# Starting places of the split weight tiles in a two-layer encoder trunk

## The chip, the core and the metric

The kernel runs on one core of a Trainium2 chip. The time is the device time of one execution in microseconds (us); the smaller the better. The core has five engines that run side by side and wait for each other through semaphores: TensorE (PE; its weight loads are shown as PEld), VectorE (DVE), ScalarE (ACT), GpSimd (POOL) and SyncE (SP), which here issues DMAs. TensorE reads its operands from SBUF, the on-chip working memory of 128 partitions, and writes to PSUM. An address below is a byte address within an SBUF partition; it is the same in all partitions.

## The reference

The reference computes a two-layer encoder on 512 tokens of width 1024 in float32. Layer 0 (A) mixes with a gated matrix memory (mLSTM, 4 heads of 192) beside cross-attention to 256 memory tokens; layer 1 (B) mixes with chunked band attention (12 heads of 64, keys and values from a projection made once after layer 0) beside the same kind of cross-attention. After each mixer comes a gated MLP of width 2816 with a causal convolution of width 3. Cut to the parts that name the weights:

```python
def conv_ffn(h, w_up, conv_w, conv_b, w_down):
    u, g = jnp.split(h @ w_up, 2, axis=-1)
    g = causal_dwconv(g, conv_w, conv_b)
    return (jax.nn.silu(g) * u) @ w_down

for l in range(DEPTH):
    h = rmsnorm(x, norm_mix_g[l])
    if l < N_A_LAYERS:
        proj = h @ a_w_in[a]        # q, k, v, o, gates, q_mem -> mlstm_chunkwise
    else:
        proj = h @ b_w_in[bl]       # q, q_mem -> band_attention over k_pad, v_pad
    mem_out = memory_attention(q_mem, mem, mem_w_kv[l])
    x = x + jnp.concatenate([mix_out, mem_out], axis=-1) @ w_out
    x = x + conv_ffn(rmsnorm(x, norm_ffn_g[l]), ...)
    if l == N_A_LAYERS - 1:
        ks_, vs_ = jnp.split(rmsnorm(x, kv_norm_g) @ w_kv, 2, axis=-1)
return rmsnorm(x, final_g)
```

## The kernel before

**Products in three parts.** Activations are kept with the features on the partitions, 512 tokens in the free dimension. Every operand of a product is split into a high part, rounded to the type fp32r, and a low part, the rest. A product is then three matmuls into one PSUM tile: high by high, low by high and high by low. `mm3` (L167 to L171) issues them; L169 reads the high part of the stationary operand with the high part of the moving one, L170 the high part with the low part of the moving one, and L171 the low part of the stationary one. Each matmul loads its stationary operand, 128 by 128, anew.

**Weight tiles.** `load` (L136) brings a block of a weight matrix of up to 128 x 1024 into a buffer `wr`, by a DMA of SP's queue. `parts` (L148) takes a buffer `wh` and a buffer `wl`, and `split` (L129) fills them: L130 casts `wr` into `wh` on ACT, and L131 subtracts `wh` from `wr` into `wl` on DVE. `halves` (L155) takes the same two buffers without filling them, where the order of the casts is written out by hand. `weights` (L160) is `load` and `parts` together. Each of the tags `wr`, `wh` and `wl` has three buffers that are used in turn, 4096 bytes a partition; a tile is taken from the start of its buffer. In the built program the first `wh` buffer starts at byte 188480, the first `wl` buffer at byte 200768, behind them come the tags `rb` (rows of the norms) and `bias`. There are 208 pairs of `wh` and `wl`.

**Who reads the tiles.** In most products the weights are the stationary operand: `project` (L173: `wh[:, k, :]` for each of 8 blocks k, 512 bytes apart), `OutProjection.part` (L614), `down_products` (L741), the key products of the memory (L353), and in the second form of the MLP `products` (L766) and `wide_products` (L780, its lines L784 and L785), which read halves of tiles that `split_up` and `split_sums` (L889, L892) made by `parts`. In `value_columns` (L979), `value_products` (L360) and the last product of the kernel (L1446 to L1466) the weights are the moving operand. In `value_columns` a tile holds two row blocks of 384 columns, or of 392 where the eight gate columns are loaded with them. The MLP also makes forms of weights in buffers of the tag `u` (L869), which has 57 buffers of 2048 bytes.

**Order.** PE, ACT and DVE run in an order written out by hand in the first stage (L422) and in the second form of the MLP (L799); elsewhere the order comes from the generators that `weave` (L200) interleaves, a filler of projections beside the steps of an attention. Tiles are planned by tag: a buffer is free again when the last reader of its former tile is done, and the engine that writes it waits for that.

Of the kernel before, what the change touches and what calls it, by code (L numbers as in the profile page):

```python
# [10 lines left out]
F32R = mybir.dt.float32r  # L11
# [5 lines left out]
P = 128  # L17
D = 1024
# [37 lines left out]
def trunk(  # L56
# [30 lines left out]
    def sb(tag, shape, dtype=F32):  # L87
        count[0] += 1
        return pool.tile(shape, dtype, tag=tag, name=f"{tag}{count[0]}", bufs=bufs[tag])

    def ps(tag):
        count[0] += 1
        return psum.tile([P, S], F32, tag=tag, name=f"p{tag}{count[0]}", bufs=pbufs[tag])
# [35 lines left out]
    def split(hi, lo, src, on_act=True, pinned=False):  # L129
        high = A.copy(hi, src) if on_act else V.tensor_copy(hi, src)  # L130
        low = V.tensor_tensor(out=lo, in0=src, in1=f(hi), op=ALU.subtract)  # L131
        if pinned:
            pin(high)
            pin(low)

    def load(src, a, b, extra=None):  # L136
# [8 lines left out]
            nc.sync.dma_start(raw[:, :, b:], extra)  # L145
        return raw

    def parts(raw, pinned=False):  # L148
        _, a, b = raw.shape
        hi = sb("wh", [P, D], F32R)[:, : a * b].rearrange("p (a b) -> p a b", a=a)  # L150
        lo = sb("wl", [P, D], F32R)[:, : a * b].rearrange("p (a b) -> p a b", a=a)
        split(hi, lo, raw, pinned=pinned)
        return hi, lo

    def halves(raw):  # L155

        _, a, b = raw.shape
        return [sb(tag, [P, D], F32R)[:, : a * b].rearrange("p (a b) -> p a b", a=a) for tag in ("wh", "wl")]

    def weights(*args):  # L160
        return parts(load(*args))

    def rows(w, c0, n, k0=0, k1=None):
        k1 = k1 if k1 is not None else w.shape[0] // P
        return w[k0 * P : k1 * P, c0 : c0 + n].rearrange("(k p) c -> p k c", p=P)
# [85 lines left out]
    class Norm:  # L251
# [14 lines left out]
        def finish(self):  # L266


            parts = [sb("t", [P, S], F32R) for _ in range(2)]
            split(*parts, self.acc)  # L270
            yield 7.4
            o = ps("sc")
            for i, part in enumerate(parts):
                nc.tensor.matmul(o, onesr, part, start=i == 0, stop=i == 1)
            v, r, t = sb("rb", [P, S]), sb("t", [P, S]), sb("t", [P, S])
            A.activation(t, o, AF.Ln, scale=1.0 / D, bias=eps)
            V.tensor_scalar(v, o, 1.0 / D, EPS, op0=ALU.mult, op1=ALU.add)
            A.activation(r, t, AF.Exp, scale=-0.5)
            A.activation(t, r, AF.Square)
            yield 4  # L280
            V.scalar_tensor_tensor(t, t, -0.5, v, op0=ALU.mult, op1=ALU.mult)
            self.row = sb("rb", [P, S])
            V.scalar_tensor_tensor(self.row, t, 1.5, r, op0=ALU.add, op1=ALU.mult)
# [138 lines left out]
    with tc.manual_schedule(engines={mybir.EngineType.PE, mybir.EngineType.Activation, mybir.EngineType.DVE}):  # L422
# [9 lines left out]
        for q in range(KT // 2 + 1):  # L432
            if q < KT // 2:
# [6 lines left out]
                hi, lo = sb("u", [P, S], F32R), sb("u", [P, S], F32R)  # L440
# [32 lines left out]
        for j in range(KT):  # L473
            G.dma_start(xspill[j], xT[j])
        norm.spread()
        vws1.append(halves(vraw1[1]))
        A.copy(vws1[1][0], vraw1[1])
        vo = two_banks("mm", "sc")
        value_products(vo, *vws1[0], 0)
        keep(1, 0, ko, A.copy)  # L480
        raw = value_weights(1, 0)
        vw = [halves(raw)]
        A.copy(vw[0][0], raw)
        x_scaled(0)
# [783 lines left out]
    for j in range(KT):  # L1268
        wh, wl = weights(rows(ffn_w_down[0], j * P, P, FT - LAST, FT), LAST, P)
        o = ps("mm")  # L1270
# [175 lines left out]
    for hf in range(2):  # L1446
# [6 lines left out]
        for Ts, pieces in groups:  # L1453
            for c in pieces:
                if c.start:
                    os_[Ts[0]] = ps("mm")
                for u in range(n):
# [3 lines left out]
                    wh, wl = ws[u]  # L1461
# [61 lines left out]
```

## Time and profile before

| | |
|---|---|
| median of 3 runs | 1194.86 us (1194.71 to 1195.16) |
| profiled execution | 1195.72 us, its span 1194.0 us |
| mean granted TensorE clock | 0.999 |
| instructions in the span | 18184 |
| matmuls | 6719 |

The span runs from the first to the last instruction of the profiled execution; the execution's own time also holds what lies around it. Lines such as L169 are line numbers of the kernel before. A group reads: line, engine, operation, output tile<-input tiles by the program's names, shape, count, then busy time and the mean ns of one, then the idle time of the engine just before and what ended it. The answers about a tile give the shortest, median and longest duration in ns of each kind of instruction that writes or reads it, and when the first and the last one started. The timeline gives start and length in us of each instruction. A row of a stretch gives, for each engine in the order PE, PEld, DVE, ACT and POOL, busy time and number of instructions, then the granted clock, the DMA share and GB/s.

### The profile page before, as it was taken

Reading aid. Unit: us, or ns where it says so; the run is one execution under the profiler, and the core shown is the slowest. Engines: PE = TensorE matmul, PEld = TensorE weight load, DVE = VectorE, ACT = ScalarE, POOL = GpSimd, SP = SyncE. Lnnn points to the kernel's source line nnn. Section 1 sums busy time; section 2 is a strip of 40 time slices with the busy share of each in tenths; the row PEclk is TensorE's granted clock in tenths of the full one; section 3 lists DMA queues with packets and bytes.
Section 4 is the critical chain, followed back from the end, with each engine's and each line's share of the span. In section 5 each row is a group of like instructions: output and inputs, shape, how many; then the busy total and the mean of one; then the engine's idle time right before and its main releaser. Section 6 shows DMA issues by size and latency. Waiting matters only on the chain.

```text
span 1194.0 us, 18184 instructions
## 1 busy us (share of the span) xinstructions
PE 1183.5 (99%) x6719; PEld 1037.0 (87%) x6719; DVE 961.7 (81%) x1760; ACT 725.2 (61%) x1294; POOL 130.3 (11%) x222
## 2 busy tenths in 40 slices
PE   9999999999999999999999999999999999999997
PEld 9988888888899998999888888888889988999986
DVE  6877788788978888888698888997896888888855
ACT  5648677655656555555576677776565655555545
POOL 1211201010021111111020000101001011011100
PEclk9999999999999999999999999999999999999999
DMA  8645313444265676665464313246336455665551
GB/s 289 212 108 140 84 54 80 152 144 141 88 156 147 156 165 165 154 144 123 142 204 123 89 54 101 69 135 185 111 99 141 116 139 135 142 141 139 119 158 71
DMA packets 200155, 158.61 MB, mean 133 GB/s; under 512 B 8344, under 2 KB 179838, under 8 KB 200066
## 3 DMA queue, kind: packets, MB, share of 16 engines
q1 hardware_dynamic: 183906, 119.74, 34.1%
q0 software_dynamic: 15584, 36.67, 14.9%
q8 instruction: 53, 0.87, 0.3%
q10 hardware_dynamic: 576, 1.05, 0.2%
q14 instruction: 36, 0.29, 0.1%
HBM read 128.89 MB, written 32.46 MB: 135 GB/s over the span
## 4 chain that ended last, share of the span: by engine, by line
PE 92%; ACT 3%; DVE 2%; DMA 1%; SPq 1%; issue 0%; POOL 0%; POOLq 0%; DVEq 0%; ACTq 0%
PE pmm L169 15%; PE pmm L170 15%; PE pmm L171 15%; PE ptr L171 6%; PE ptr L169 6%; PE ptr L170 6%; PE pmm L785 6%; PE psc L171 5%; PE psc L170 5%; PE psc L169 5%; PE pmm L784 3%; PE psc L519 2%; PE ptr L1350 1%; DMA wr<-in_mem_w_kv_dram 1%; PE ptr L1371 1%; PE ptr L1372 1%
## 5 line engine op out<-in xcount | busy, mean ns | idle before, releaser
L169 PE MATMUL pmm<-u,wh 128*128 128x512 f32 (+1 forms) x872 | 309.1, 355 | 0.3 <-ACT u L130 0.2
L170 PE MATMUL pmm<-u,wh 128*128 128x512 f32 (+1 forms) x872 | 306.2, 351 | 0.0
L171 PE MATMUL pmm<-u,wl 128*128 128x512 f32 (+1 forms) x872 | 306.0, 351 | 0.0
L131 DVE TENSOR_TENSOR wl<-wr,wh 128x1024 fp32r<-128x1024 f32 (+3 forms) x172 | 199.8, 1163 | 57.0 <-ACT wh L130 55.0
L130 ACT CAST wh<-wr 128x1024 fp32r<-128x1024 f32 (+3 forms) x172 | 172.4, 1004 | 97.7 <-PE pmm L170 44.5
L171 PEld LDWEIGHTS pmm<-u,wl 128*128 128x128 f32 x872 | 164.5, 189 | 21.1
L169 PEld LDWEIGHTS pmm<-u,wh 128*128 128x128 f32 x872 | 164.5, 189 | 18.5 <-ACT u L130 1.1
L170 PEld LDWEIGHTS pmm<-u,wh 128*128 128x128 f32 x872 | 164.7, 189 | 18.2 <-DVE u L131 0.5
L169 PE MATMUL ptr<-u,wh 128*128 128x512 f32 x272 | 106.7, 392 | 0.0
L171 PE MATMUL ptr<-u,wl 128*128 128x512 f32 x272 | 106.1, 390 | 0.0
L753 POOL DMA_DIRECT2D xspill<-t x64 | 55.6, 869 | 461.1 <-ACT t L752 450.4
L170 PE MATMUL ptr<-u,wh 128*128 128x512 f32 x272 | 105.9, 389 | 0.0
L130 ACT CAST u<-pt 128x512 fp32r<-128x512 f32 x102 | 63.0, 620 | 46.8 <-DVE pt L875 46.7
L131 DVE TENSOR_TENSOR u<-pt,u 128x512 fp32r<-128x512 f32 x102 | 69.9, 688 | 11.2 <-ACT u L130 8.5
L169 PE MATMUL psc<-u,wh 128*128 128x256 f32 (+1 forms) x232 | 76.1, 328 | 0.0
L171 PE MATMUL psc<-u,wl 128*128 128x256 f32 (+1 forms) x232 | 75.9, 327 | 0.0
L170 PE MATMUL psc<-u,wh 128*128 128x256 f32 (+1 forms) x232 | 75.9, 327 | 0.0
L937 ACT ACTIVATE t<-t 128x512 f32<-128x512 f32 x34 | 21.6, 634 | 79.3 <-DVE t L660 79.3
L785 PE MATMUL pmm<-u,u 128*128 128x512 f32 x192 | 69.6, 397 | 0.0
L821 DVE TENSOR_TENSOR t<-t,pmm 128x256 f32<-128x256 f32 x72 | 30.2, 419 | 44.9 <-ACT t L819 44.8
L752 ACT COPY t<-ptr 128x512 f32<-128x512 f32 x64 | 37.4, 585 | 43.1 <-PE ptr L171 43.1
L660 DVE SCALAR_TENSOR_TENSOR t<-t,cols,t 128x511 f32<-128x511 f32 x80 | 59.7, 746 | 3.7 <-ACT t L667 3.7
(300 smaller groups left out, 2673.8 us busy)
## 6 DMA issues: line engine op xcount, KB each, us to landing
wr<-in_ffn_w_up_dram SPq DMA_DIRECT2D x54, 512.0 KB, 4.2
wr<-in_ffn_w_down_dram SPq DMA_DIRECT2D x38, 512.0 KB, 4.1
pt<-in_ffn_w_up_dram SPq DMA_DIRECT2D x34, 512.0 KB, 6.2
xspill<-t POOLq DMA_DIRECT2D x64, 256.0 KB, 5.2
wr<-in_a_w_in_dram SPq DMA_DIRECT2D x20, 512.0 KB, 3.7
xspill<-u POOLq DMA_DIRECT2D x32, 256.0 KB, 2.6
u<-xspill SPq DMA_DIRECT2D x32, 256.0 KB, 5.0
wr<-in_w_kv_dram SPq DMA_DIRECT2D x12, 512.0 KB, 3.7
```

The costliest lines, as they stand in the source:

```text
L130: high = A.copy(hi, src) if on_act else V.tensor_copy(hi, src)
L131: low = V.tensor_tensor(out=lo, in0=src, in1=f(hi), op=ALU.subtract)
L169: nc.tensor.matmul(o, lh, rh, start=first, stop=False, skip_group_check=more)
L170: nc.tensor.matmul(o, lh, rl, start=False, stop=False, skip_group_check=more)
L171: nc.tensor.matmul(o, ll, rh, start=False, stop=last, skip_group_check=more)
L519: nc.tensor.matmul(o, a, b, start=first and i == 0, stop=i == 1)
L660: V.scalar_tensor_tensor(acc[:, n:], src[:, : S - n], self.fw[:, c * FT + j : c * FT + j + 1], acc[:, n:], op0=ALU.mult, op1=ALU.add,)
L752: A.copy(t, o)
L753: G.dma_start(xspill[j], t, accum_op=ALU.add)
L784: nc.tensor.matmul(r[:, :H], w[1][:, k], p[i - 1][:, :H], start=False, stop=False, skip_group_check=True)
L785: nc.tensor.matmul(r, w[0][:, k], p[i - 1], start=False, stop=k == n - 1, skip_group_check=True)
L821: V.tensor_tensor(out=o, in0=o, in1=r[:, H:], op=ALU.add)
```

## The change

The buffers of `wh` and `wl` grow by 64 elements, 256 bytes. A counter `turn` numbers the pairs as the program is written down, i = 0, 1, 2 and so on. The high part of pair i starts 8 x (i mod 8) elements, that is 32 x (i mod 8) bytes, behind the start of its buffer, and the low part 32 x ((i + i // 8) mod 8) bytes. For the first eight pairs both have the same place; from each group of eight to the next the low part moves on by one place against the high part. What is computed, and with which instructions, stays as it was.

```diff
+    turn = [0]
+
+    def weight_tiles(a, b):
+        i = turn[0]
+        turn[0] += 1
+        places = (8 * (i % 8), 8 * ((i + i // 8) % 8))
+        return [
+            sb(tag, [P, D + 64], F32R)[:, o : o + a * b].rearrange("p (a b) -> p a b", a=a)
+            for tag, o in zip(("wh", "wl"), places)
+        ]
+
     def parts(raw, pinned=False):
         _, a, b = raw.shape
-        hi = sb("wh", [P, D], F32R)[:, : a * b].rearrange("p (a b) -> p a b", a=a)
-        lo = sb("wl", [P, D], F32R)[:, : a * b].rearrange("p (a b) -> p a b", a=a)
+        hi, lo = weight_tiles(a, b)
         split(hi, lo, raw, pinned=pinned)
         return hi, lo
 
     def halves(raw):
 
         _, a, b = raw.shape
-        return [sb(tag, [P, D], F32R)[:, : a * b].rearrange("p (a b) -> p a b", a=a) for tag in ("wh", "wl")]
+        return weight_tiles(a, b)
```

## The prediction

> **What bounds the kernel now.** I read the page's busy times first, then its clock row and chain, then the matmuls in order of time, and last the rows of the two engines that write the weight tiles.
>
> ```profile
> span 1194.0 us, 18184 instructions
> PE 1183.5 (99%) x6719; PEld 1037.0 (87%) x6719; DVE 961.7 (81%) x1760; ACT 725.2 (61%) x1294; POOL 130.3 (11%) x222
> PEclk9999999999999999999999999999999999999999
> PE 92%; ACT 3%; DVE 2%; DMA 1%; SPq 1%; issue 0%; POOL 0%; POOLq 0%; DVEq 0%; ACTq 0%
> ```
>
> TensorE is busy from end to end at a fully granted clock, and 92% of the chain that ended last is its work. The time therefore changes by what a matmul costs; the 5% of ACT and DVE is the second place to look.
>
> A busy row counts pipelined matmuls twice, so the price of one is the step from its start to the next start. The timeline of a stretch in which nothing else delays TensorE gives it: first and last of 28 matmuls of 512 columns, and first and last of 11 of 256 columns.
>
> ```profile
> 599.80 0.39 PE L169 MATMUL pmm<-u,wh 128*128 128x512 f32 x1
> ...
> 605.92 0.39 PE L169 MATMUL pmm<-u,wh 128*128 128x512 f32 x1
> ```
>
> ```profile
> 523.49 0.28 PE L170 MATMUL psc<-u,wh 128*128 128x256 f32 x1
> ...
> 524.69 0.28 PE L171 MATMUL psc<-u,wl 128*128 128x256 f32 x1
> ```
>
> 6.12 us over 27 steps is 226.7 ns; 1.20 us over 10 steps is 120.0 ns. The 256 columns between them cost 106.7 ns, or 0.417 ns each, so a matmul costs its columns plus a fixed 13.3 ns (226.7 less 512 x 0.417), as much as 32 columns. The first stretch runs beside busy neighbours:
>
> ```profile
> 600.00:650.00 50.00, 50.00 (x231) 41.52 (x230) 42.86 (x76) 32.18 (x58) 7.95 (x15) 1.00 0.53 165
> ```
>
> In these 50 us DVE is busy 42.86 us and ACT 32.18 us, DMA 53%, and the step of 226.7 ns holds through the quoted part without one late matmul. So whatever TensorE's reads share with the other engines costs nothing there, at phases that drift by themselves. What stays is the relation inside one instruction, or between a matmul and the weight load beside it, where both run in step: that is what an address can change.
>
> **The change part by part.**
>
> Instructions: none is added, removed or moved. In the built program each engine has the same instructions in the same order with the same waits, DMA issues of SP and POOL included; only addresses differ. So no queue is passed, nothing new waits, and this part costs 0.
>
> Places: today every wh, wl, wr and u tile starts 64 bytes past a multiple of 512. Afterwards the buffers are 256 bytes longer, and tile i starts 32 x (i mod 8) bytes later, so each place holds an eighth of the 208 tiles. The tiles behind, rb and bias, move by 1536 bytes, three times 512: the same remainder, cost 0, DMAs into bias included. No DMA reads or writes wh or wl.
>
> Weight reads: the rows that count who reads the tiles, as stationary operand first (L171 reads wl as often as L169 and L170 read wh), then as moving operand (again three lines each).
>
> ```profile
> L169 PEld LDWEIGHTS pmm<-u,wh x872: 186/188/192, 19.6 to 1146.1; 128*128 128x128 f32 x175
> L169 PEld LDWEIGHTS ptr<-u,wh x272: 187/188/192, 242.3 to 1135.6; 128*128 128x128 f32 x136
> L169 PEld LDWEIGHTS psc<-u,wh x232: 187/188/192, 281.4 to 1144.6; 128*128 128x128 f32 x116
> L785 PEld LDWEIGHTS pmm<-u,wh x96: 187/188/192, 401.2 to 1133.4; 128*128 128x128 f32 x96
> L784 PEld LDWEIGHTS pmm<-u,wl x96: 189/191/192, 401.1 to 1133.2; 128*128 128x128 f32 x96
> ...
> L170 PEld LDWEIGHTS pmm<-wl,u x80: 187/188/192, 30.6 to 1186.5; 128*128 128x128 f32 x80
> L170 PEld LDWEIGHTS psc<-wl,u x42: 187/188/192, 31.0 to 1177.8; 128*128 128x128 f32 x42
> L170 PEld LDWEIGHTS ptr<-wl,u x12: 187/188/192, 1178.4 to 1184.3; 128*128 128x128 f32 x12
> ```
>
> That is 3 x (872 + 272 + 232) + 2 x 96 = 4320 loads, and 3 x (80 + 42 + 12) = 402 matmuls that stream a weight tile. A load takes 188 ns but loads follow each other every 120 ns in the 256-column stretch, so most of it is covered by the matmuls; what can be exposed is the fixed 13.3 ns.
>
> The moving reads have a test in the trace. In the value columns with gates (392 columns), the second row block of a tile starts 392 x 4 = 1568 bytes in, three times 512 and 32 more: exactly the shift that the change makes. The first 12 matmuls read the block at the usual place, the next 12 the shifted one.
>
> ```profile
> 36.40 0.34 PE L169 MATMUL pmm<-wh,u 128*128 128x392 f32 x1
> ...
> 38.53 0.34 PE L169 MATMUL pmm<-wh,u 128*128 128x392 f32 x1
> ...
> 40.66 0.34 PE L169 MATMUL pmm<-wh,u 128*128 128x392 f32 x1
> ```
>
> 2.13 us for either dozen, 177.5 ns each, against 392 x 0.417 + 13.3 = 176.7 ns by the two stretches above. A moving row off by 32 bytes costs nothing, to the 0.01 us that the rows resolve: 0.01 / 12 = 0.8 ns a matmul, so 402 of them lie within 0.3 us either way. I take 0.
>
> No stationary row starts at an odd multiple of 32 bytes today, so the 4320 loads are bounded by the fixed part. Suppose the 13.3 ns is a read of the weight row in units. A row of 128 words is 512 bytes. If the unit is 64 bytes, the row takes 8 units at today's place and 9 at the four odd places: 13.3 / 8 = 1.67 ns on half the loads, 2160 x 1.67 = 3.6 us more. If the unit is 128 bytes, today's row (64 past) touches 5, and at the two places that are 64 or 192 bytes along it touches 4: 13.3 / 5 = 2.67 ns less on 1080 loads, 2.9 us less. If it is 32 bytes or less, nothing changes. I take 0, because the nearest row, the 32-byte shift of the other operand, is at 0, and keep -2.9 and +3.6 us.
>
> The Trainium skill, page "SBUF — State Buffer", section "Door 1: The DMA port swizzle", has lines of 16 bytes in this memory. By it all eight places are alike, and the sum would be 0; no run here shows it for a stationary read.
>
> Writes of ACT and DVE: each of the 208 tiles is written by a cast and a subtraction.
>
> ```profile
> L131 DVE TENSOR_TENSOR wl<-wr,wh 128x1024 fp32r<-128x1024 f32 x143 | 174.9, 1223 | 49.2 <-ACT wh L130 47.3
> L130 ACT CAST wh<-wr 128x1024 fp32r<-128x1024 f32 x143 | 150.3, 1053 | 78.8 <-PE pmm L170 37.9 <-PE psc L171 16.5 <-issue 9.1
> L131 DVE TENSOR_TENSOR u<-pt,u 128x512 fp32r<-128x512 f32 x102 | 69.9, 688 | 11.2 <-ACT u L130 8.5
> L130 ACT CAST u<-pt 128x512 fp32r<-128x512 f32 x102 | 63.0, 620 | 46.8 <-DVE pt L875 46.7
> L660 DVE SCALAR_TENSOR_TENSOR t<-t,cols,t 128x511 f32<-128x511 f32 x40 | 29.8, 746 | 3.7 <-ACT t L667 3.7
> L660 DVE SCALAR_TENSOR_TENSOR t<-t,cols,t 128x510 f32<-128x510 f32 x40 | 29.8, 745 | 0.0
> L302 DVE SCALAR_TENSOR_TENSOR u<-u,cols,u 128x512 fp32r<-128x512 f32 x32 | 23.5, 749 | 0.0
> ```
>
> From 512 to 1024 columns DVE pays (1223 - 688) / 512 = 1.045 ns a column and ACT 0.846 ns; the operands all have one remainder now. The taps of L660 run their output 4 and 8 bytes off the first source and take 746 and 745 ns, against 749 ns for the aligned 512 columns of L302. So operands out of step cost DVE nothing, and I take 0 for both engines. For the bounds I let them be 1% slower or faster throughout: TensorE's work covers that, except in ACT's and DVE's 5% of the chain, 59.7 us, of which 1% is 0.6 us either way.
>
> The sum: 1194.0 us of span plus 1.7 us around it, the 1195.7 us of the profiled execution, plus 0. The median of the runs shown, 1194.86 us, lies 0.9 us below that execution, so the forecast for a run is 1194.9, said as **1195.0 us**. Its own bounds are -2.9 - 0.3 - 0.6 = -3.8 us (1191.1) and +3.6 + 0.3 + 0.6 = +4.5 us (1199.4).
>
> **The rivals.**
>
> 1. Slower: the common start avoids a collision. Load and matmul run side by side, both from remainder 64; at one of the eight distances their reads might fall on the same part of the memory and the load's fixed 13.3 ns be paid twice. 4320 / 8 x 13.3 = 7.2 us: 1202.1 us. It decides (0.2% is 2.4 us) from 0.55 ns a load on the mean. For it: the distance between the two reads is what the change varies most. Against it: the 392-column rows try distances 0 and 32 bytes and find no difference. The 64-byte unit above is the milder kin of this, at 1198.5 us.
>
> 2. Faster: the fixed 13.3 ns is itself such a collision, because all starts share a remainder, and seven places of eight are rid of it: 4320 x 7/8 x 13.3 = 50.3 us, 1144.6 us. For it: 13.3 ns is a large constant, on every matmul quoted. Against it: the block at 32 bytes' distance pays it in full (177.5 ns against 163.3 without it). Milder, the 128-byte unit gives 1192.0 us.
>
> The Trainium skill, "TensorE: Matmul & The Clock Gate", section "Back-to-back issue gap", puts the step at N/2.4 + 2.5 ns, 215.8 ns for 512 columns. The trace differs by 10.9 ns; an estimate with that page's constant, were the rest a collision, is 4320 x 7/8 x 10.9 = 41 us less. No run here tells what the rest is.
>
> 3. That the change does not act as said (the tile planner waits otherwise) is ruled out by the equal order and waits, and has no chance of its own.
>
> **How the numbers follow.** No change from the places, 1195.0 us: 0.52. Slower by units of 64 bytes: 0.15; by a collision: 0.12. Faster by units of 128 bytes: 0.14; by a collision removed, in whole or in part: 0.07. Of the time, 0.2% is what a measurement of this kernel can tell from no change. This gives faster 0.21, same 0.52, slower 0.27. I lean no further to "same" because the stationary read, the largest count, has no row. The range reaches from the sum's low end, 1191, to the collision's 1202.1 with 0.9 us of small terms, 1203; the removed collision and worse meetings than one place in eight stay out, a little over 1 in 10. The likeliest case alone has 1192.5 to 1197.3.
>
> **What would show it.** Right: steps of 226.7 and 120.0 ns in the same two stretches of the changed kernel, loads at 188 ns, L131 near 1223 and L130 near 1053 ns for 1024 columns. Wrong on the loads: steps that differ from tile to tile with the place, an eighth or a half of them longer by some nanoseconds. Wrong on ACT and DVE: equal steps, but longer L130 or L131 and later matmuls in the attention stages, where they wait for those engines. It fails outright if the fixed 13.3 ns shrinks or doubles at some places.

## The result and the profile after

The changed kernel takes 1202.24 us (median of 3 runs, 1202.0 to 1204.0) against 1194.86 us: 7.4 us more, a ratio of 1.0066 with a 95% interval of 1.005 to 1.0082. It is slower by 0.7%, little, but clear of the spread of the runs. The profiled execution took 1204.0 us, its span 1202.2 us, so that span is 8.2 us longer than that of before.

The page of the changed kernel, with the same four rows that the prediction began with:

```profile
span 1202.2 us, 18184 instructions
PE 1191.0 (99%) x6719; PEld 1033.5 (86%) x6719; DVE 962.7 (80%) x1760; ACT 723.5 (60%) x1294; POOL 130.3 (11%) x222
PEclk9999999999999999999999999999999999999999
PE 96%; DMA 2%; ACT 1%; DVE 1%; SPq 0%; issue 0%; POOL 0%; POOLq 0%
```

Instructions, counts and clock are the same, DVE, ACT and POOL are as busy as before (962.7 against 961.7, 723.5 against 725.2, 130.3 in both), and TensorE's share of the chain has grown from 92% to 96%. So it is not that TensorE waits longer for the others; it takes longer for the same 6719 matmuls. The steps say so directly. The timeline of the changed kernel in a stretch of projections beside an attention, first and last of 23 matmuls of 512 columns (what was L169 to L171 is now L179 to L181, all ten lines later):

```profile
600.69 0.39 PE L181 MATMUL pmm<-u,wl 128*128 128x512 f32 x1
...
605.81 0.40 PE L179 MATMUL pmm<-u,wh 128*128 128x512 f32 x1
```

5.12 us over 22 steps is 232.7 ns, where it was 226.7 ns. Not all stages pay this. Two stretches of the kernel before, then the same two of the changed one (the row gives PE's busy time and matmuls first); 260 to 340 us is a run of 512-column matmuls, 420 to 560 us is the second form of the MLP, where matmuls of 256 and of 512 columns are mixed:

```profile
260.00:340.00 80.00, 80.00 (x354) 66.20 (x353) 72.51 (x117) 48.43 (x76) 4.66 (x8) 1.00 0.41 120
420.00:560.00 140.00, 140.00 (x871) 126.19 (x870) 115.78 (x182) 78.61 (x135) 22.77 (x30) 1.00 0.64 151
```

```profile
260.00:340.00 80.00, 80.00 (x347) 64.87 (x346) 72.62 (x118) 48.33 (x78) 4.68 (x8) 1.00 0.39 121
420.00:560.00 140.00, 140.00 (x874) 125.68 (x873) 115.82 (x183) 79.20 (x137) 22.85 (x30) 1.00 0.65 152
```

In the first, TensorE starts 347 matmuls in the time of 354; in the second it starts as many as before. The wide matmuls of the MLP (L785 before, L795 now) mark both ends of that stage in each layer; first start and last start of a layer's 96, before and then after:

```profile
L785 PE MATMUL pmm<-u,u x96: 387/396/403, 395.7 to 576.5; 128*128 128x512 f32 x96
...
L785 PE MATMUL pmm<-u,u x96: 387/396/403, 956.9 to 1137.7; 128*128 128x512 f32 x96
```

```profile
L795 PE MATMUL pmm<-u,u x96: 387/396/403, 400.3 to 581.2; 128*128 128x512 f32 x96
...
L795 PE MATMUL pmm<-u,u x96: 390/395/404, 964.5 to 1145.4; 128*128 128x512 f32 x96
```

The stage takes 180.8 us before and 180.9 us after, in either layer. In this stage two effects cancel. Worked out from the starts in the two traces, in the first layer, with the split weights as stationary operand: the 276 steps from a matmul of 512 columns to the next of 512 rise from 228.7 to 231.9 ns on the mean (0.9 us), and the 408 steps from 256 columns to 256 fall from 119.8 to 117.9 ns (0.8 us). Over the whole span the same count gives 9.9 us more on 2580 steps of 512 columns, 0.6 us more on 119 steps of 512 columns that read the weights as moving operand, and 2.3 us less on 1381 steps of 256 columns; all other steps together come out even. That makes the 8.2 us.

By place in the span, the 8.2 us are lost outside this stage: 4.6 us ahead of it in the first layer (395.7 to 400.3), 2.9 us between the two (380.4 us from 576.5 to 956.9, 383.3 us from 581.2 to 964.5), 0.5 us behind the second, and the two times 0.1 us inside.

### The profile page after: what moved, and what is told of

Its sections match the earlier page's. It is cut to its first block, busy times and chain, and to the rows that moved or that the text cites. A ratio compares the mean times of both kernels' runs of the same rounds, so it can differ in the third digit from the quotient of the medians.

```text
span 1202.2 us, 18184 instructions
## 1 busy us (share of the span) xinstructions
PE 1191.0 (99%) x6719; PEld 1033.5 (86%) x6719; DVE 962.7 (80%) x1760; ACT 723.5 (60%) x1294; POOL 130.3 (11%) x222
## 4 chain that ended last, share of the span: by engine, by line
PE 96%; DMA 2%; ACT 1%; DVE 1%; SPq 0%; issue 0%; POOL 0%; POOLq 0%
PE pmm L179 16%; PE pmm L180 15%; PE pmm L181 15%; PE ptr L180 6%; PE ptr L181 6%; PE ptr L179 6%; PE pmm L795 6%; PE psc L180 5%; PE psc L181 5%; PE psc L179 5%; PE pmm L794 3%; PE psc L529 2%; DMA wr<-in_mem_w_kv_dram 2%; PE ptr L1360 1%; PE ptr L1381 1%; PE ptr L1382 1%
## 5 line engine op out<-in xcount | busy, mean ns | idle before, releaser
L179 PE MATMUL pmm<-u,wh 128*128 128x512 f32 (+1 forms) x872 | 310.1, 356 | 0.1
L181 PE MATMUL pmm<-u,wl 128*128 128x512 f32 (+1 forms) x872 | 307.2, 353 | 0.0
L181 PEld LDWEIGHTS pmm<-u,wl 128*128 128x128 f32 x872 | 164.0, 188 | 23.0
L179 PEld LDWEIGHTS pmm<-u,wh 128*128 128x128 f32 x872 | 164.1, 188 | 20.1 <-ACT u L130 1.0
L179 PE MATMUL ptr<-u,wh 128*128 128x512 f32 x272 | 107.5, 395 | 0.0
L181 PE MATMUL ptr<-u,wl 128*128 128x512 f32 x272 | 107.3, 394 | 0.0
L179 PE MATMUL psc<-u,wh 128*128 128x256 f32 (+1 forms) x232 | 76.3, 329 | 0.0
L181 PE MATMUL psc<-u,wl 128*128 128x256 f32 (+1 forms) x232 | 76.0, 327 | 0.0
L795 PE MATMUL pmm<-u,u 128*128 128x512 f32 x192 | 69.5, 396 | 0.0
```

The lines of the kernel that those rows point to most:

```text
L179: nc.tensor.matmul(o, lh, rh, start=first, stop=False, skip_group_check=more)
L181: nc.tensor.matmul(o, ll, rh, start=False, stop=last, skip_group_check=more)
L795: nc.tensor.matmul(r, w[0][:, k], p[i - 1], start=False, stop=k == n - 1, skip_group_check=True)
```

## The experiments

Distance, below, is the start of the stationary tile less the start of the moving one, as remainders of 512 bytes. Before the change every `wh`, `wl` and `u` tile has the remainder 64, so the distance is 0; the change makes it 32 bytes times the place, and in every other buffer 256 bytes more, because the buffers are 256 bytes longer (e1 prices these). The places below leave the 256 bytes out. Unless a diff says otherwise, an experiment is the changed kernel with another line for the places, in elements of 4 bytes: `places = (8 * (i % 8), 8 * ((i + i // 8) % 8))`. The excess of a step is taken over 226.7 ns. Each run was compared with the kernel before on the same chip. The expectations call the theories by letters; theory A is that the distance between the two operands of a matmul lengthens its step.

**e1_longer_only.** The longer buffers alone, every tile at the start of its own.

```diff
-        places = (8 * (i % 8), 8 * ((i + i // 8) % 8))
+        places = (0, 0)
```

> The buffers of wh and wl are 256 bytes longer, every tile starts at place 0. Theory A (distance: a weight load's read meets the read of the matmul beside it, by the distance between the two starting addresses): as before, 1194.9 us, steps of 226.7 ns in the plain stage. Theory B (succession: it costs that one load starts at another place than the load before it): 1194.9 us. Theory C (the buffers' new spacing or the moved rb and bias tiles do it): 1202 us.

Measured: 1195.79 us, before 1195.39, ratio 1.0002 [0.9993, 1.0011]. Longer buffers, and `rb` and `bias` in other places, cost nothing beyond the 0.1% of the interval; theory C falls. Since the buffers are 256 bytes longer, some of these tiles start 320 past a multiple of 512 instead of 64. The timeline of this run, first and last of 15 matmuls, gives 3.17 us over 14 steps, 226.4 ns: a distance of 256 bytes acts like none.

```profile
602.76 0.39 PE L179 MATMUL pmm<-u,wh 128*128 128x512 f32 x1
...
605.93 0.39 PE L181 MATMUL pmm<-u,wl 128*128 128x512 f32 x1
```

**e2_all_one.** All tiles 32 bytes on, without any turn from pair to pair.

```diff
+        places = (8, 8)
```

> Every tile, high and low, starts 32 bytes behind the start of its buffer. Theory A: all 4320 loads have a distance of 32 bytes, slower by what that one distance costs, 1198 to 1204 us; steps in the plain stage above 229 ns. Theory B: places never change, 1194.9 us and 226.7 ns. Theory C: 1202 us.

Measured: 1205.44 us, ratio 1.0084 [1.0069, 1.0099]. One constant distance of 32 bytes costs 10.0 us, more than the changing distances of the change; theory B falls. Its timeline, first and last of 15 matmuls:

```profile
602.66 0.40 PE L181 MATMUL pmm<-u,wl 128*128 128x512 f32 x1
...
605.93 0.40 PE L180 MATMUL pmm<-u,wh 128*128 128x512 f32 x1
```

3.27 us over 14 steps, 233.6 ns; from the unrounded starts in the trace it is 233.3 ns, 6.67 ns above 226.7. In units of the prediction's 0.417 ns a column, a step is 560 columns long instead of 544: 16 more. Its row for the mixed stage has 870 matmuls, against 871 before:

```profile
420.00:560.00 140.00, 140.00 (x870) 125.28 (x870) 115.20 (x181) 78.80 (x138) 22.79 (x30) 1.00 0.65 151
```

**e3_no_drift.** High and low part of a pair at one place, which turns through eight.

```diff
+        places = (8 * (i % 8), 8 * (i % 8))
```

> High and low part of a tile start at the same place, which moves by 32 bytes from tile to tile. Theory A: the distances are spread over the eight places as in the changed kernel, 1201 to 1203 us. Theory B: in the plain stage one load in 24 starts at a new place instead of two in three, so a sixteenth of the loss, 1195.4 us.

Measured: 1203.1 us, ratio 1.0063 [1.0048, 1.0078], as the change itself, so the drift of the low part is not what costs. Three tiles that follow each other in its timeline, at places 7, 0 and 1, first and last matmul of each tile's 24:

```profile
299.61 0.40 PE L179 MATMUL pmm<-u,wh 128*128 128x512 f32 x1
...
304.98 0.39 PE L181 MATMUL pmm<-u,wl 128*128 128x512 f32 x1
305.21 0.39 PE L179 MATMUL psc<-u,wh 128*128 128x512 f32 x1
...
310.42 0.40 PE L181 MATMUL psc<-u,wl 128*128 128x512 f32 x1
310.66 0.39 PE L179 MATMUL pmm<-u,wh 128*128 128x512 f32 x1
...
316.02 0.39 PE L181 MATMUL pmm<-u,wl 128*128 128x512 f32 x1
```

23 steps take 5.37, 5.21 and 5.36 us: 233.5, 226.5 and 233.0 ns. Here the step changes with the tile, at its first matmul. Worked out from the starts in the trace for the tiles between 260 and 330 us and between 825 and 895 us, the mean excess of a tile is 6.3 to 7.4 ns at places 1 to 5 and 7, 2.7 to 3.1 ns at place 6 (192 bytes), and -0.1 to 1.3 ns at place 0. The 1.3 ns belong to the tile from 853.12 us: there the steps are irregular for seven matmuls before they are 226.7 ns again.

**e4_low_only.** Only the low part off, so that one load in three has a distance.

```diff
+        places = (0, 8)
```

> High parts at place 0, low parts 32 bytes behind. Theory A: a third of the loads have the distance, a third of what the run with all tiles at 32 bytes loses. Theory B: two of three loads start at another place than the one before, the whole loss, 1200 to 1202 us.

Measured: 1204.29 us, ratio 1.0082 [1.0065, 1.0099]. Theory A's third of the cost is wrong: one load in three costs as much as all three. Its timeline, first three and last of 13 matmuls:

```profile
602.75 0.40 PE L179 MATMUL pmm<-u,wh 128*128 128x512 f32 x1
602.98 0.40 PE L180 MATMUL pmm<-u,wh 128*128 128x512 f32 x1
603.22 0.39 PE L181 MATMUL pmm<-u,wl 128*128 128x512 f32 x1
...
605.55 0.40 PE L179 MATMUL pmm<-u,wh 128*128 128x512 f32 x1
```

2.80 us over 12 steps is 233.3 ns. The two steps with distance 0 do not fall back to 226.7 ns between the ones that have a distance. The change shows the same: its two parts mostly stand at different places, and a tile whose high part is at place 0 still steps at 230.3 ns (24 matmuls from 307.23 us) and 230.5 ns (from 854.96 us).

**e5_all_shifted.** The kernel before, with 32 bytes taken in front of everything, so that all tiles, stationary and moving, start 32 bytes later.

```diff
+    V.memset(cpool.tile([P, 8], F32, name="front"), 0.0)
     ident = cpool.tile([P, P], F32, name="ident")
```

> The kernel before with a constant of 32 bytes in front of all tiles: every tile of the kernel, weights and activations alike, starts 32 bytes later, so the distances between a load and the matmul beside it stay 0. Theory A (distance): 1194.9 us and 226.7 ns. Theory D (the place itself: a row that starts 96 instead of 64 bytes past a multiple of 256 reads worse): 1205 us like the run with all weight tiles at 32 bytes, or worse, because the activations are off too.

Measured: 1195.11 us, before 1195.54, ratio 0.9996 [0.9986, 1.0005]. First and last of 15 matmuls in its timeline (mm3 is at L170 to L172 here):

```profile
602.78 0.39 PE L171 MATMUL pmm<-u,wh 128*128 128x512 f32 x1
...
605.95 0.39 PE L170 MATMUL pmm<-u,wh 128*128 128x512 f32 x1
```

3.17 us over 14 steps, 226.4 ns. A common shift of 32 bytes is free; the same 32 bytes between the operands (e2) are not. Theory D falls.

**e6_sixteen.** Sixteen places 16 bytes apart, one run, as a scan over the distance.

```diff
+        places = (4 * (i % 16), 4 * (i % 16))
```

> High and low part of tile i both start 16 x (i mod 16) bytes behind the start of their buffers, a scan of the distance by 16 bytes in one trace, read tile by tile in the plain stages. Theory A with a fixed price: 226.7 ns at 0, 233.3 ns at every other distance, 16 bytes too. Rival, units of 32 bytes or more: 16 bytes costs what 0 costs. A third outcome, a curve: the step grows with the distance and falls towards 256 bytes, where 192 bytes (229 ns so far) is on the way down.

Measured: 1201.61 us in one run, before 1195.54. Mean excess per tile of the 512-column stages, by distance. Each mean rests on a few tiles, and tiles of one distance can differ: at 240 bytes one had 0.9 and one 2.4 ns.

| bytes | ns | bytes | ns |
|---|---|---|---|
| 0 | 0.35 | 128 | 6.7 |
| 16 | 0.35 | 144 | 6.8 |
| 32 | 6.3 | 160 | 6.9 |
| 48 | 6.6 | 176 | 3.45 |
| 64 | 6.4 | 192 | 2.9 |
| 80 | 5.1 | 208 | 5.1 |
| 96 | 7.3 | 224 | 6.6 |
| 112 | 6.5 | 240 | 1.7 |

A tile at 16 bytes and the next at 32, in its timeline, first and last matmul of each:

```profile
310.47 0.39 PE L179 MATMUL pmm<-u,wh 128*128 128x512 f32 x1
...
315.68 0.40 PE L181 MATMUL pmm<-u,wl 128*128 128x512 f32 x1
315.92 0.39 PE L179 MATMUL psc<-u,wh 128*128 128x512 f32 x1
...
321.28 0.39 PE L181 MATMUL psc<-u,wl 128*128 128x512 f32 x1
```

5.21 us over 23 steps (226.5 ns), then 5.36 us (233.0 ns). By this scan 16 bytes looked free; e10 and e11 below show that it is not always. The matmuls of 256 columns differ: their step of 120.0 ns was shortest at 192 bytes, 113.3 ns, and at the other distances beside 0 it was 0.1 to 3.7 ns under 120.0.

**e7_up_six and e8_up_sums_six.** That last reading was put to use: tiles that matmuls of 256 columns read are moved, by 192 bytes, in the second form of the MLP; all others stay at distance 0. e7 moves the tiles of `split_up`, which only such matmuls read. e8 moves those of `split_sums` as well, and the high parts of these are also read by 48 matmuls of 512 columns a layer, in `wide_products`.

```diff
+    def weight_tiles(a, b, place=0):
+        places = (place, place)
...
+    def parts(raw, pinned=False, place=0):
+        hi, lo = weight_tiles(a, b, place)
...
-            self.a11, self.a12 = zip(*(self.halves(t) for t in parts(self.up)))
+            self.a11, self.a12 = zip(*(self.halves(t) for t in parts(self.up, place=48)))
```

```diff
-            self.s1, self.s3 = zip(*(self.halves(t) for t in parts(self.s13)))
+            self.s1, self.s3 = zip(*(self.halves(t) for t in parts(self.s13, place=48)))
```

> Only the tile of the up weights in the second form of the MLP (32 a layer and a half: 17 in each layer) starts 192 bytes behind its buffer's start, all others at 0. In the run without drift its 24 matmuls of 256 columns took 113.4 ns at this place and 120.0 ns at place 0. If that is a gain: 34 steps x 24 x 6.6 ns = 5.4 us less, 1189.5 us. Rival: the neighbours give it back, as the steps of that stage took 15.4 to 15.5 us at every place: 1194.9 us.

> As the run before, and the tile of the sums (s1 and s3) starts at 192 bytes too: another 12 matmuls of 256 columns. If the gain holds there, 34 x 12 x 6 ns = 2.4 us more, 1187 us; if the neighbours of 512 columns pay for it (s3 is read by the wide products too), 1190 us or more.

Measured: e7 1192.96 us, ratio 0.9979 [0.997, 0.9989]; e8 1190.19 us, before 1195.54, ratio 0.9956 [0.9941, 0.9971]. e7 brought 2.6 us, half of the 5.4 us expected: its moved matmuls step at about 118 ns, not 113. In e8 the first moved tile of the stage (24 matmuls from 391.55 us) has 113.3 ns, the ones behind it 117.8; why was not tried. e8 is 5.4 us faster than the kernel before on its chip. The timeline of e8 (mm3 is at L175 to L177, `wide_products` at L790 and L791), first and last of 15 matmuls of 256 columns, and its rows for the two stretches and for the wide matmuls:

```profile
514.29 0.28 PE L175 MATMUL pmm<-u,wh 128*128 128x256 f32 x1
...
515.94 0.28 PE L177 MATMUL pmm<-u,wl 128*128 128x256 f32 x1
```

```profile
260.00:340.00 80.00, 80.00 (x354) 66.20 (x353) 72.22 (x116) 48.19 (x76) 4.88 (x8) 1.00 0.41 119
420.00:560.00 140.00, 140.00 (x879) 126.46 (x878) 115.81 (x182) 79.57 (x138) 23.62 (x31) 1.00 0.64 151
```

```profile
L791 PE MATMUL pmm<-u,u x96: 395/398/403, 394.4 to 574.0; 128*128 128x512 f32 x96
...
L791 PE MATMUL pmm<-u,u x96: 395/398/403, 953.2 to 1132.8; 128*128 128x512 f32 x96
```

1.65 us over 14 steps is 117.9 ns against 120.0; the plain stretch has its 354 matmuls, and the mixed stage 879 where it had 871. From first to last wide matmul the stage takes 179.6 us instead of 180.8, in both layers, which makes 2.4 us. Of the other 2.6 us of the span (1194.0 to 1189.0 us), 1.3 us come ahead of the first such stage and 1.2 us between the two (379.2 us for 380.4).

**e9_forms_zero and e9_forms_six.** e8, with the forms that the MLP makes in buffers of `u` put into eight buffers of their own (`u` keeps 49 of its 57), once at distance 0, and once 192 bytes on by a pad in front of them.

```diff
-    bufs = {"wr": 3, "wh": 3, "wl": 3, "u": 57, "t": 8, ...}
+    bufs = {"wr": 3, "wh": 3, "wl": 3, "u": 49, "f": 8, "z": 1, "t": 8, ...}
...
-            hi, lo = (sb("u", [P, S], F32R).rearrange("p (a b) -> p a b", a=KT // 2) for _ in range(2))
+            hi, lo = (sb("f", [P, S], F32R).rearrange("p (a b) -> p a b", a=KT // 2) for _ in range(2))
```

```diff
+            if self.l == 0:
+                sb("z", [P, 48])
```

> As the run with up and sums tiles at 192 bytes, but the forms of the second MLP part (s2, a22, s4) get eight buffers of their own, taken from the 57 of u; they still start at distance 0. It is the comparison for the next run. If the 49 buffers left to u suffice, 1190 us; if attention then waits for buffers, more.

> The same with the forms' buffers 192 bytes further on, so their loads have a distance of 192 bytes too. Theory A holds for any stationary operand, not for the split weight tiles alone: the 24 loads of forms a step beside matmuls of 256 columns then cost some 3 ns less each, 34 x 24 x 3 ns = 2.4 us less than the run before. Rival: only the tiles of wh and wl behave so, or the neighbours give it back: no difference.

Measured: 1195.0 us, before 1195.23, ratio 0.9993 [0.9984, 1.0003], and 1196.6 us, ratio 1.0008 [0.9998, 1.0017]. The wide matmuls of e9_forms_zero:

```profile
L791 PE MATMUL pmm<-u,f x96: 395/398/403, 394.3 to 573.9; 128*128 128x512 f32 x96
...
L791 PE MATMUL pmm<-u,f x96: 395/398/403, 958.6 to 1138.2; 128*128 128x512 f32 x96
```

Its mixed stage is e8's, 179.6 us, but the second one begins at 958.6 us where e8's begins at 953.2: this division of the buffers costs 5.4 us in what lies between. That it is the eight fewer for `u` which do so is likely, but was not tried by itself. For e9_forms_six the same rows begin and end at 394.3 and 574.2 us, 179.9 us: moving the forms, too, gains nothing.

**e10_low_sixteen and e11_all_sixteen.** Is 16 bytes really free? The low part alone 16 bytes off, then both parts.

```diff
+        places = (0, 4)
```

```diff
+        places = (4, 4)
```

> The low parts start 16 bytes behind their buffers' starts, the high parts at 0. Theory A with the curve of the scan (16 bytes costs what 0 costs): 1194.9 us, 226.7 ns, where 32 bytes in the same place cost 9 us. Rival (any distance in one of three loads breaks the beat): 1201 to 1204 us.

> High and low parts alike start 16 bytes behind their buffers' starts. With the scan (a tile with both parts at 16 bytes ran at 226.7 ns): 1195 us, and what the run with the low parts alone at 16 bytes lost is due to the distance changing from load to load. Rival (the scan's tiles at 16 bytes were carried by their neighbours at 0, and 16 bytes costs like 32): 1200 us or more.

Measured: e10 1201.21 us, before 1195.23, ratio 1.0048 [1.0033, 1.0063]; e11 1204.51 us, before 1194.87, ratio 1.008 [1.0063, 1.0097]. e10, first and last of 13 matmuls, then e11 in two stretches, 24 matmuls and 23:

```profile
602.84 0.40 PE L181 MATMUL pmm<-u,wl 128*128 128x512 f32 x1
...
605.62 0.40 PE L181 MATMUL pmm<-u,wl 128*128 128x512 f32 x1
```

```profile
262.71 0.39 PE L179 MATMUL pmm<-u,wh 128*128 128x512 f32 x1
...
267.92 0.39 PE L181 MATMUL pmm<-u,wl 128*128 128x512 f32 x1
...
302.71 0.40 PE L180 MATMUL pmm<-u,wh 128*128 128x512 f32 x1
...
307.85 0.39 PE L181 MATMUL psc<-u,wl 128*128 128x512 f32 x1
```

e10 steps at 2.78 / 12 = 231.7 ns. e11 has both steps at one and the same distance: 5.21 / 23 = 226.5 ns in the first stretch, 5.14 / 22 = 233.6 ns in the second. The turn comes at about 284 us, and from there on the stretch stays slow; the second layer repeats it at about 849 us. Ahead of the turn stand a few matmuls of another kind. At the same spot the kernel before is out of step, too, for six matmuls from 280.90 us, and is then back at 226.7 ns. So at 16 bytes a run of matmuls keeps the step that it has, the fast one or the slow one. By this reading, e6's tile at 16 bytes was fast because the tile ahead of it was.

## Why the prediction was wrong, though the time lies in its range

**The number.** 1202.24 us lies between the stated 1191 and 1203, but not for the reason given. The likeliest case, no change from the places at 1195.0 us with a chance of 0.52, failed, and the sum's own upper end, 1199.4, was passed. The range covers the result only because it was drawn out to the first rival's 1202.1, which had a chance of 0.12; that this size fits to 0.2 us is luck, as shown below.

**Instructions and places.** Right: the same instructions, and e1 gives the longer buffers and moved rows their price of 0. The prediction overlooked that the longer buffers by themselves start every other buffer 256 bytes further on; by e1 that costs nothing either.

**Writes of ACT and DVE, loads, waits.** Right. In the changed kernel, by rows that answer to those of the prediction:

```profile
L795 PEld LDWEIGHTS pmm<-u,wh x96: 187/188/193, 405.8 to 1141.1; 128*128 128x128 f32 x96
...
L131 DVE TENSOR_TENSOR wl<-wr,wh 128x1024 fp32r<-128x1024 f32 x143 | 174.9, 1223 | 50.9 <-ACT wh L130 49.1
L130 ACT CAST wh<-wr 128x1024 fp32r<-128x1024 f32 x143 | 149.6, 1048 | 87.5 <-PE pmm L180 41.1 <-PE psc L181 16.9 <-issue 10.8
```

1223 ns as before, 1048 ns for 1053, and a load is 188 ns long. The length of a load shows nothing of the loss; the step from start to start does. ACT waits 41.1 us for `pmm` where it waited 37.9, being ahead of a slower TensorE.

**Moving reads.** As predicted for the 392 columns, but not for all 402 matmuls: the 119 steps of 512 columns took 0.6 us more, twice the 0.3 us allowed. At 392 columns the two dozens still take 2.12 and 2.13 us:

```profile
37.51 0.34 PE L179 MATMUL pmm<-wh,u 128*128 128x392 f32 x1
...
39.63 0.34 PE L179 MATMUL pmm<-wh,u 128*128 128x392 f32 x1
...
41.76 0.34 PE L179 MATMUL pmm<-wh,u 128*128 128x392 f32 x1
```

**Weight reads: the step that failed.** The prediction took the stationary reads at 0 "because the nearest row, the 32-byte shift of the other operand, is at 0", with bounds of -2.9 and +3.6 us. The change as a whole measured +7.4 us, and by the sums over the traces nearly all of it is this term. The row was sound but did not carry over: it tests matmuls of 392 columns with the weights as moving operand, and the loss lies in runs of 512-column matmuls, most of them with the weights as stationary operand. It is the width that makes the row blind, not the role of the operand. The last product of the kernel reads the weights as moving operand with 512 columns. First and last of 66 matmuls of it that follow each other, in the kernel before and then in e2, where the weights alone are 32 bytes off (as they are the moving operand here, the distance is -32):

```profile
1150.96 0.40 PE L169 MATMUL pmm<-wh,u 128*128 128x512 f32 x1
...
1165.72 0.40 PE L171 MATMUL psc<-wh,u 128*128 128x512 f32 x1
```

```profile
1159.97 0.40 PE L179 MATMUL pmm<-wh,u 128*128 128x512 f32 x1
...
1175.14 0.39 PE L181 MATMUL psc<-wh,u 128*128 128x512 f32 x1
```

14.76 us over 65 steps is 227.1 ns, 15.17 us is 233.4 ns: the moving operand off by 32 bytes costs at 512 columns what the stationary one does. At 384 columns it costs nothing: from the starts in the trace, 54 matmuls of the value columns take 9.27 us from first to last before (from 61.77 us) and 9.27 us in e2 (from 60.90 us). With the change's several distances they take 9.35 us (from 62.96 us), 1.5 ns a step more.

The bounds were worked out from the start of a weight row alone, in units of 64 or 128 bytes. e5 shows that this was the wrong variable: moving everything by 32 bytes costs nothing, and only the distance to the moving operand counts. By the 64-byte unit half of the places would have paid 1.67 ns; in e3 six of eight pay 6.3 to 7.4 ns and a seventh about 2.8.

The prediction used the 16-byte lines of the Trainium skill, "SBUF — State Buffer", "Door 1: The DMA port swizzle", for a sum of 0 with all eight places alike. The runs differ: places 0 and 1 of e3 step at 226.5 and 233.0 ns.

**The rivals.** The first had the size (1202.1 us) and the right variable, the distance between the two reads, but not the picture. It let one distance of eight pay 13.3 ns; in fact nearly every distance but 0 pays half of that, 6.67 ns, and one load in three is enough (e4). Its 7.2 us is 13.3 ns on an eighth of all 4320 loads; the traces have 3.9 ns more on the mean 512-column step and 1.7 ns less on the mean 256-column step, and these happen to add up to nearly the same. The second, that the fixed 13.3 ns is itself a collision, falls for the 512 columns: no distance in e6 has a mean step under 226.7 ns. It has a small truth for the 256 columns, where e8 took 5.4 us off. The sign that the prediction named for an error in the loads, steps that differ from tile to tile by some nanoseconds, is what e3 shows; in the change itself the drift of the low part blurs it.

The prediction's 10.9 ns come from the formula N/2.4 + 2.5 ns of the Trainium skill, "TensorE: Matmul & The Clock Gate", "Back-to-back issue gap". That section gives it for an isolated matmul and not for a stream with weight loads, so the 10.9 ns were no sign of a collision in the 226.7 ns.

**What stays open.** Shown is when the longer step occurs; what in the reads makes it is not. The Trainium skill, "TensorE: Matmul & The Clock Gate", "Step-by-step: what each phase is for", gives TensorE separate read ports for the load and the streaming operand, so that a load takes no bandwidth from the running matmul. The relative distance of the two operands costs 2.9% of a step here (233.3 against 226.7 ns), so they are not independent in these runs; whether they meet in the memory or in TensorE itself was not tried, nor why 512 columns lose, 384 hardly do and 256 gain.

## What to carry to other kernels

Where matmuls of 512 columns and their weight loads follow each other without a gap, keep the stationary and the moving tile at the same remainder (of 256 bytes, as e1 shows); for another width, measure, because at 256 columns 192 bytes apart was better here. Look at the step from start to start: the 188 ns of a load did not move, and the recorded length of a matmul hardly did (the median of the `ptr` matmuls of L169, now L179, went from 389 to 395 ns). A row that tests a shift at one width is no price for another width; when a term rests on such a row, its bound should be at least the whole fixed part of the step. A place that looks free in a scan has to be run alone, because here a tile seems to have inherited the step of the one ahead of it.

## What the runs showed of the hardware

- The step of a 512-column matmul, as a mean over a run of them, mostly has one of two values, 226.7 or 233.3 ns, 544 or 560 times the 0.417 ns of a column. The excess of about 3 ns at 176 and 192 bytes, and e10's 231.7 ns, lie between them and were not taken apart.
- At distance 0 the fast step comes back, with the first matmul of a tile (e3, 305.21 us) or after seven (e3, 853.12 us); at 32 to 160 bytes the tiles of e6 keep a mean excess of 5 to 7 ns; and at 16 bytes either step lasts (e11).
- Which of the two operands is off does not matter at 512 columns (e2: 233.3 ns with the weights stationary, 233.4 ns with the weights moving). At 384 columns these 32 bytes cost nothing (9.27 us for 53 steps in both kernels).
- For 256 columns the best distance was another one: 113.3 ns at 192 bytes in the scan, 117.9 ns in e8, against 120.0 ns at 0. In columns, 120.0 and 113.3 ns are 288 and 272: 16 fewer, as the slow step of 512 columns is 16 more. With two groups of tiles moved there, the kernel runs in 1190.19 us, faster than both kernels of this study; the change costs 0.7%, this placement gains 0.4%.
